# Pairing the jobs on both sides of a change of token halves, asking for sums a step ahead, and landing the first gated sums in a freed quarter

## The chip, the cores and the metric

The kernel runs on one core of a Trainium2 chip. The metric is the device time of one execution in microseconds (us), as the median of several executions. Before the change it is 2456.3 us, median of 3 (2455.7 to 2457.65).

## What is computed

One decoder block on x of shape (2048, 1024), everything in float32. A normalized and modulated h goes through one projection `z = h @ w_in`, whose columns are split into two branches. Branch A takes two column blocks a and b, forms `u = a * sigmoid(b)`, runs a causal depthwise convolution of 31 taps over the tokens, a layer norm and a SiLU, and multiplies by a gate. Branch B is windowed attention with three dilations, whose outputs are merged by weights, multiplied by a gate `silu(g_attn)` and projected by `w_attn_out`. Both branches are projected to 1024 channels, merged by sigmoid gates from further columns of z, projected by `w_out`, and added to x.

```python
z = h @ w_in
a, b, g_conv, q, k, v, g_attn, m_conv, m_attn = split(z)
u = silu(layer_norm(depthwise_causal_conv(a * sigmoid(b)))) * silu(g_conv)
o = merge(dilated_window_attention(q, k, v)) * silu(g_attn)
y = sigmoid(m_conv) * (u @ w_conv_out) + sigmoid(m_attn) * (o @ w_attn_out)
x = x + gate * (y @ w_out)
```

## The kernel before, in words

Every float32 product is made of three matmuls: each operand is split into a high part (`nc.scalar.activation(h, raw, AF.Copy)` on ACT, rounded) and a low part (raw minus high, on DVE or POOL), and high*high, high*low and low*high are added in PSUM. h itself is kept as 16 quarter tiles, a high and a low part of 4 blocks of 128 channels by 512 tokens each, named by channel half kh and token quarter t (`quarter_tile`, L224). They lie in two pools: t = 0 in a pool that lives to the end, t > 0 in one that is closed after the quads.

Four stages follow one another. The order of PE's instructions is written out by hand. The other engines' instructions are ordered by a scheduler that follows the program order as a priority but runs an instruction earlier where its inputs and its buffer are there; at run time each engine and each DMA queue works strictly in the order that came out. All DMAs concerned here are issued by SP.

1. Attention units (`project_step`, up to 1093 us).
2. Merge steps (the loop `for step, (half, j) in enumerate(order)`, L842, up to about 1211 us): 32 steps of 24 matmuls into `pzg` (L367), with the gate on ACT and DVE (`sg`, L510, L511), weights and sums of the attention outputs (`om`, L505, L507), a product on POOL (`sg`, L512), and a transpose on PE one or two steps later (`pta`, L517). In the last twelve steps, 32 pieces of 256 tokens of precomputed sums (S2, S3, S4, S1, from `s_d`) are also loaded into `raw`, a tag with three buffers, and split into the quarters of h that are no longer needed (`quarter_place`: load L830, high part on ACT L836, low part on DVE or POOL L837).
3. Quads (`quad`, `ab_quad`, `gate_quad`, about 1211 to 1987 us): a Strassen-like scheme, seven products in place of eight. There are 20 jobs for each half of the tokens; each has 7 products of 12 matmuls of 512 columns (L958), each from its own quarter (A11, A12, S2, S1, S3, S4, A22, in this order). PSUM sums go out through `kept` (ACT, L964, into one of eight scratch buffers), additions on DVE (L971, L985) and POOL (L982), and a sink: a gate job applies its function on ACT and writes to DRAM (L1081, L1082); its last result goes through a tile `gt` of which there are three. An ab job writes `ut`, from which the convolution is computed by DVE in 49 parts (`conv_parts`), taken from the list `conv_todo` by `run_conv`. The weights of the next job (`column_steps`: four loads `wB`, differences on POOL L922, high parts L927, low parts L928) are made one step per product, seven products ahead. In the last job of the first half the seven quarters are reloaded one by one: after product n, quarter n of the second half is asked for in four pieces of 512 tokens (`landing`: three pieces in the `gt` buffers and one in `ld`, or, for every other quarter, four in scratch), and split one product later. `load_wa` loads and splits the attention output weights in the last job, through `fraw`, two buffers.
4. The attention output projection `ya` (32 blocks of 12 matmuls, L1185), then the convolution branch `yc` and the output. The first block needs the four gated sums of the first 512 tokens (`ai_0`, `load_ai(0, k)`, L1261); before, they are loaded after the quads' pools are closed, through raw buffers that lie where the convolution's tiles were, and through one `gt` buffer.

Of the kernel before, what the change touches and what calls it, by code (L numbers as in the profile page):

```python
# [10 lines left out]
F32 = mybir.dt.float32  # L11
F32R = mybir.dt.float32r
# [42 lines left out]
def tile_hybrid_block(  # L55
# [168 lines left out]
    def quarter_tile(kh, t, hl, name, dtype=F32R):  # L224

        return hpools[t > 0].tile([P, 4, 512], dtype, tag=f"h{hl}{kh}{t}", name=name)

# [610 lines left out]

    def quarter_place(*args):
        quarter_load(*args[:5])  # L840
        quarter_split(*args)

    placing = [(n, k, c) for n in ("S2", "S3", "S4", "S1") for k in range(4) for c in (0, 256)]
    wts = [cur, None]
# [30 lines left out]
    ws = wpool_c.__enter__()  # L875
    wraw_c = tc.tile_pool(name="wr", bufs=7, side="right", reuse_waits="tile")
    wr = wraw_c.__enter__()
# [14 lines left out]

    def scratch(n=None):

        i = turn_of[0] % 8 if n is None else (turn_of[0] - 1) // 4 * 4 % 8 ^ 4 | n
        if n is None:
            turn_of[0] += 1
        return spares[i // 4][:, i % 4]

    def landing(i):  # L900

        if i % 8 >= 4:
            return scratch(i % 4)
        own, tag = (gp, "gt") if i % 8 < 3 else (cv, "ld")
        return own.tile([P, 512], F32, tag=tag, name=f"landing{i}", bufs=3 if tag == "gt" else 1)

# [40 lines left out]

    def quad(name, got, sink, after):

# [18 lines left out]
        s1 = kept(pa)  # L968
        after(0)
        product(1, pb)  # L970
        nc.vector.tensor_tensor(s1, s1, pb, op=ALU.add)  # L971
        sink(0, 0, s1)
        after(1)
        product(2, pa, True)
        s2 = kept(pa)
        after(2)
        product(3, pc, True)
        s5 = kept(pc)
        after(3)
# [3 lines left out]
        after(4)  # L983
# [4 lines left out]
        after(5)  # L988
        product(6, pa)
        sink(1, 0, pa)  # L990
        after(6)

    def conv_parts(half, cb, ut):

        e, o, both = ut[:, 0], ut[:, 1], cv.tile([P, 528], F32, tag="us", name=f"us{half}_{cb}")
        box = {}
# [26 lines left out]
        def join():  # L1023
            y = box["y"] = cv.tile([P, 512, 2], F32, tag="ca", name=f"ca{half}_{cb}")
            nc.vector.tensor_add(y[:, 1:, 0], box["e"][:, 1:], box["o"][:, :511])
# [7 lines left out]
        def mixed(j):  # L1033
            def f():
                dst = box["y"][:, :, 1] if j == HT else box["e"]
                stt(dst, both[:, 1 + j : 513 + j], pair_taps[:, cb, j : j + 1], box["e"], op0=ALU.mult,  # L1036
                    op1=ALU.subtract if j == 0 else ALU.add)
            return f
# [9 lines left out]

        nc.gpsimd.tensor_add(both[:, 1:], e[:, 1:], o[:, 1:])
        if half == 0:  # L1050
            nc.gpsimd.tensor_copy(tail[:, cb], ut[:, :, 513:528])
        return [*[even(j) for j in range(HT + 1)], *[odd(j) for j in range(HT)], join,
                *[mixed(j) for j in range(HT + 1)], done]

    def ab_quad(half, cb, got, after):
        ut = cv.tile([P, 2, 528], F32, tag="ut", name=f"ut{half}_{cb}")
# [16 lines left out]

        quad(f"ab{half}_{cb}", got, sink, after)

    def gate_quad(half, dst, func, cb, got, after):
        def sink(t, col, z):
# [5 lines left out]

        quad(f"g{half}_{dst.name}_{cb}", got, sink, after)

# [36 lines left out]

    got, steps = job_columns(0)
    for f in steps:
        f()
    held = []
    for i, (kind, half, g, cb) in enumerate(jobs):
        last_of_half = i + 1 < len(jobs) and jobs[i + 1][1] > half
        nxt, steps = job_columns(i + 1) if i + 1 < len(jobs) else ([], [])
        if i + 1 == len(jobs):  # L1130
            run_conv(len(conv_todo))

        def after(n):
            if steps:
                steps[n]()
            for f in held:
                f()
            held.clear()
            if last_of_half:
                name = PRODUCTS[n][0]  # L1140
                for k in range(4):
                    args = 1, name, k, slice(0, 512), landing(4 * n + k)
                    quarter_load(*args)
                    held.append(lambda args=args, k=k: quarter_split(*args, nc.gpsimd if k == 3 else nc.vector))
            else:
                run_conv(3 if n < 5 else 4)
            if i + 1 == len(jobs) and 0 < n <= NH:
                load_wa(n - 1)

        if kind is ab_quad:  # L1150
            ab_quad(half, cb, got, after)
        else:
            gate_quad(half, g[1], g[2], cb, got, after)
        got = nxt
    cv_c.__exit__(None, None, None)
# [104 lines left out]

    ais = {}  # L1261

    def load_ai(t, k):
        ais[t, k] = parts(t // 2, f"ai{t}_{k}")
        raw = gp.tile([P, 512], F32, tag="gt", name="airaw") if t == 0 and k == 3 else None
        split_big(*ais[t, k], ai_d[k, :, 512 * t : 512 * t + 512], raw=raw)

# [6 lines left out]
    def load_wc0(k):  # L1274
        load_wc(0, k, *(wcp.tile([P, 512], F32R, name=f"wc0{hl}{k}") for hl in "hl"))

    for k in range(NH):
        load_ai(0, k)
# [126 lines left out]
```

## Time and profile before

| | us |
|---|---|
| median of 3 executions | 2456.3 |
| the profiled execution: device time | 2458.03 |
| its span, first to last instruction | 2455.9 |
| PE busy | 2401.1 (98%) |
| DVE busy | 1702.4 (69%) |
| ACT busy | 970.0 (39%) |
| POOL busy | 833.3 (34%) |
| merge steps 20 to 31 with their tail, about | 1161 to 1211 |
| quads | 1211 to 1987 |

PE is the engine that is busy nearly all the time, so the time is the sum of its work and its idle pieces; a matmul of 512 columns is issued every 0.23 us at the full clock. The granted clock of PE is a share of 2.4 GHz; 0.5 is the lower of its two levels.

### The profile page before, as it was taken

How to read it: one execution, taken by the hardware profiler on the slowest of the kernel's cores; microseconds unless marked ns; L12 is line 12 of the kernel's file. 1: busy time of each engine (PE TensorE's matmuls, PEld its weight loads, DVE VectorE, ACT ScalarE, POOL GpSimd, SP SyncE). 2: the span in 40 equal slices, each digit the busy share in tenths (PEclk: the TensorE clock that was granted, in tenths of full speed). 3: DMA queues.
4: the chain of work that ended last, by engine and by line, in shares of the span. 5: the costliest groups of instructions: out<-in, count | busy, mean ns of one | idle time of the engine just before them, and what ended most of it. 6: DMA issues, size and time to landing. Idle time of an engine off the chain costs nothing.

```text
span 2455.9 us, 39171 instructions
## 1 busy us (share of the span) xinstructions
PE 2401.1 (98%) x12881; PEld 2140.9 (87%) x12881; DVE 1702.4 (69%) x3916; ACT 970.0 (39%) x2738; POOL 833.3 (34%) x954
## 2 busy tenths in 40 slices
PE   6999999999999999999899999999999999999999
PEld 2989999999999999999788888778888878888887
DVE  5855655555556555557599999999999967874333
ACT  4733433343344344335444444544444434431000
POOL 4421111111111111112486777787777710000000
PEclk8999999999999999999999999999999999999999
DMA  7633543454452221126623332542333279866343
GB/s 255 216 110 109 164 122 100 148 147 144 144 148 81 69 80 49 31 59 190 186 90 99 95 103 90 169 145 86 108 95 96 98 278 315 269 198 221 121 147 101
DMA packets 329737, 336.26 MB, mean 137 GB/s; under 512 B 27512, under 2 KB 251032, under 8 KB 329534
## 3 DMA queue, kind: packets, MB, share of 16 engines
q1 hardware_dynamic: 327758, 331.07, 42.9%
q10 hardware_dynamic: 1776, 2.69, 0.3%
q8 instruction: 103, 1.69, 0.3%
q14 instruction: 100, 0.82, 0.1%
HBM read 216.01 MB, written 117.64 MB: 136 GB/s over the span
## 4 chain that ended last, share of the span: by engine, by line
PE 89%; DMA 3%; ACT 2%; DVE 1%; POOL 1%; issue 1%; SPq 0%; DVEq 0%; POOLq 0%; ACTq 0%
PE pz L367 30%; PE yc L1185 7%; PE out L1185 7%; PE paab L958 7%; PE ya L1185 4%; PE pcab L958 4%; PE pag_mc_d L958 4%; PE pag_g_d L958 4%; PE pag_ma_d L958 3%; PE ps L439 3%; PE po L458 3%; PE pcg_g_d L958 2%; PE pcg_mc_d L958 2%; PE ptq L429 2%; PE pzg L367 2%; PE pbab L958 2%
## 5 line engine op out<-in xcount | busy, mean ns | idle before, releaser
L367 PE MATMUL pz<-wh_u,hT_lo 128*128 128x384 f32 x1536 | 538.5, 351 | 4.9 <-DVE hT_lo L286 2.7
L367 PE MATMUL pz<-wh_u,hT_hi 128*128 128x384 f32 x1536 | 519.6, 338 | 6.3 <-ACT wh_u L343 3.3
L367 PE MATMUL pz<-wl_u,hT_hi 128*128 128x384 f32 x1536 | 520.4, 339 | 0.5 <-DVE wl_u L346 0.4
L395 DVE SCALAR_TENSOR_TENSOR qk<-pz,st,wqk 128x128 f32<-128x128 f32 x384 | 117.0, 346 | 319.9 <-POOL st L111 319.7
L110 POOL TENSOR_SCALAR st<-st 128x2 f32<-128x2 f32 x192 | 48.1, 251 | 815.5 <-ACT sq L384 815.5
L367 PEld LDWEIGHTS pz<-wh_u,hT_hi 128*128 128x128 f32 x1536 | 291.7, 190 | 9.0 <-ACT wh_u L343 4.0
L367 PEld LDWEIGHTS pz<-wh_u,hT_lo 128*128 128x128 f32 x1536 | 290.1, 189 | 8.0 <-DVE hT_lo L286 3.5
L367 PEld LDWEIGHTS pz<-wl_u,hT_hi 128*128 128x128 f32 x1536 | 290.6, 189 | 2.1 <-DVE wl_u L346 1.6
L431 ACT ACTIVATE qkT<-ptq 128x256 f32<-128x256 f32 x192 | 73.6, 383 | 420.6 <-PE ptq L429 420.0
L928 POOL TENSOR_TENSOR slT<-wB,shT 128x512 fp32r<-128x512 f32 x120 | 163.1, 1367 | 55.8 <-ACT shT L927 55.8
L1036 DVE SCALAR_TENSOR_TENSOR ce<-us,pair_taps,ce 128x512 f32<-128x512 f32 x240 | 179.6, 749 | 1.5
L1007 DVE SCALAR_TENSOR_TENSOR ce<-ut,chan,ce 128x512 f32<-128x512 f32 x240 | 179.3, 747 | 0.0
L1020 DVE SCALAR_TENSOR_TENSOR cq<-ut,chan,cq 128x512 f32<-128x512 f32 x208 | 156.3, 752 | 3.8
L384 ACT ACTIVATE sq<-pz 128x128 bf16<-128x128 f32 x384 | 106.0, 276 | 100.8 <-PE pz L367 93.9
L111 POOL TENSOR_TENSOR st<-st,mhalf 128x2 f32<-128x2 f32 x192 | 136.5, 711 | 16.0
L927 ACT ACTIVATE shB<-wB 128x512 fp32r<-128x512 f32 x120 | 75.6, 631 | 155.6 <-issue 111.7
L922 POOL TENSOR_TENSOR wB<-wB,wB 128x512 f32<-128x512 f32 x80 | 105.0, 1313 | 45.3 <-DVE slB L928 40.4
L444 ACT ACTIVATE sm<-sm,osb 128x128 f32<-128x128 f32 (+1 forms) x192 | 88.7, 462 | 62.4 <-DVE osb L442 59.6
L927 ACT ACTIVATE shT<-wB 128x512 fp32r<-128x512 f32 x120 | 75.1, 626 | 87.5 <-PE pcab L958 24.4
L1368 DVE TENSOR_TENSOR ot<-out,gate_row 128x512 f32<-128x512 f32 x32 | 22.1, 692 | 116.2 <-PE out L1185 116.2
L458 PE MATMUL po<-lv,pT 128*128 128x128 f32 x600 | 97.3, 274 | 0.0
L458 PEld LDWEIGHTS po<-lv,pT 128*128 128x128 f32 x600 | 93.1, 189 | 0.5 <-issue 0.5
(610 smaller groups left out, 6336.6 us busy)
## 6 DMA issues: line engine op xcount, KB each, us to landing
wB<-in_w_in_dram SPq DMA_DIRECT2D x160, 256.0 KB, 3.4
qkv_d<-qkv SPq DMA_DIRECT2D x128, 192.0 KB, 2.3
raw_u<-in_w_in_dram SPq DMA_DIRECT2D x93, 192.0 KB, 2.8
lqk<-qkv_d SPq DMA_DIRECT2D x128, 128.0 KB, 2.3
acc_d<-osb SPq DMA_DIRECT2D x192, 65.0 KB, 1.7
at<-acc_d SPq DMA_DIRECT2D x64, 195.0 KB, 3.9
wada<-in_w_ada_dram SPq DMA_DIRECT2D x16, 512.0 KB, 8.4
lv<-qkv_d SPq DMA_DIRECT2D x128, 64.0 KB, 1.9
```

The lines of the kernel that those rows point to most:

```text
L111: nc.gpsimd.tensor_tensor(dst, scratch[:, :n], mhalf[:, :n], op=ALU.pow)
L367: nc.tensor.matmul(pz[:, :width], part(a, k, P * j, P), w[:, :width], start=(m == 0), stop=(m == 23))
L384: nc.scalar.activation(sq, pz[:, P * i : P * i + P], AF.Square, scale=1.0 / math.sqrt(P), accum_out=st[:, i : i + 1])
L395: nc.vector.scalar_tensor_tensor(qk[:, 2 * i : 2 * i + 2].rearrange("p a b -> p (a b)"), pz[:, P * i : P * i + P], st[:, 2 + i : 3 + i], w ...
L458: nc.tensor.matmul(po[:, :P], box["pT"][:, P * i : P * i + P], vt, start=(i == 0), stop=(i == nk - 1))
L927: nc.scalar.activation(h, q[name], AF.Copy)
L928: eng.tensor_tensor(l, q[name], h.bitcast(F32), op=ALU.subtract)
L958: nc.tensor.matmul(ps, w, x, start=(m == 0 and ps.name not in first), stop=(m == 11 and not more), skip_group_check=True)
L1007: stt(box["e"], e[:, 1 + j : 513 + j], chan[:, cb, 2 * j : 2 * j + 1], box["e"], op0=ALU.mult, op1=ALU.add)
L1020: stt(box["o"], o[:, 2 + j : 514 + j], w, psum_o, op0=ALU.mult, op1=ALU.add)
L1036: stt(dst, both[:, 1 + j : 513 + j], pair_taps[:, cb, j : j + 1], box["e"], op0=ALU.mult, op1=ALU.subtract if j == 0 else ALU.add)
L1185: nc.tensor.matmul(pz, w, xx, start=(m == 0), stop=(m == len(terms) - 1))
```

## The change

- `quarter_tile` puts the quarter (kh, t) = (0, 2) into the pool that lives to the end.
- Merge steps: `quarter_place` is taken apart. Each of the steps 19 to 30 only loads its pieces, into `raw` (three buffers, odd steps) or into a new tag `sl` (three buffers, even steps); the split comes in the following step, after that step's `merge_step`.
- Quads: jobs 18 and 19 (the last two of the first half) and jobs 20 and 21 (the first two of the second) run in pairs, product by product: product 0 of both, product 1 of both, and so on. `quad` becomes a generator, `prepare` makes weight steps seven slots ahead in the new order, raw weight buffers go from 7 to 10. In job 19 the quarters are loaded after each of its products, all through the three `gt` buffers and `ld`, and split two slots later. The other jobs stay single. `run_conv` takes 2 parts per slot in the first pair, elsewhere 3 or 4. `us` and `ca` of the convolution have one buffer in place of two, and the sum for `us` becomes a part of its own.
- The first gated sums `ai0` are loaded in the last job, after products 3 to 6, through `fraw`, into the quarter of S2; `wc0` k = 4 to 7 later uses the same quarter, in place of own tiles.

```diff
-        if step >= 20:
-            for i, (n, k, c0) in enumerate([placing.pop(0) for _ in range(3 if step < 28 else 2)]):
-                raw = wp.tile([P, 384], F32, tag="raw", name=f"raw{n}_{k}_{c0}", bufs=3)[:, :256]
-                quarter_place(0, n, k, slice(c0, c0 + 256), raw, nc.vector if i < 2 else nc.gpsimd)
+        landed, landing = landing, []
+        if 19 <= step < 31:
+            for i, (n, k, c0) in enumerate([placing.pop(0) for _ in range(3 if step < 27 else 2)]):
+                if step % 2:
+                    raw = wp.tile([P, 384], F32, tag="raw", name=f"raw{n}_{k}_{c0}", bufs=3)[:, :256]
+                else:
+                    raw = wk.tile([P, 256], F32, tag="sl", name=f"sl{n}_{k}_{c0}", bufs=3)
+                landing.append((0, n, k, slice(c0, c0 + 256), raw))
+                quarter_load(*landing[-1])
...
         turns += merge_step(half, j, pz, state)
+        for i, args in enumerate(landed):
+            quarter_split(*args, nc.vector if i < 2 else nc.gpsimd)
...
+    def load_ai0(k):
+
+        if k == 0:
+            big["ai0"] = [quarter_tile(0, 2, hl, f"ai0{hl}") for hl in ("hi", "lo")]
+        ais[0, k] = [x[:, k] for x in big["ai0"]]
+        split_big(*ais[0, k], ai_d[k, :, :512])
...
+    for group in [*[[i] for i in range(half_jobs - 2)], [half_jobs - 2, half_jobs - 1], [half_jobs, half_jobs + 1],
+                  *[[i] for i in range(half_jobs + 2, len(jobs))]]:
+        slots += [(i, n) for n in range(7) for i in group]
...
+    for at, (i, n) in enumerate(slots):
+        if n == 0:
+            kind, *job = jobs[i]
+            running[i] = kind(*job, columns[i][0])
+        next(running[i], None)
+        prepare(at + 7)
+        while held and held[0][0] <= at:
+            held.pop(0)[1]()
+        if i == half_jobs - 1:
+            for k in range(4):
+                own, tag = (gp, "gt") if k < 3 else (cv, "ld")
+                raw = own.tile([P, 512], F32, tag=tag, name=f"landing{n}_{k}", bufs=3 if k < 3 else 1)
+                args = 1, PRODUCTS[n][0], k, slice(0, 512), raw
+                quarter_load(*args)
+                held.append((at + 2, lambda args=args, k=k: quarter_split(*args, nc.gpsimd if k == 3 else nc.vector)))
+        run_conv(2 if half_jobs - 2 <= i < half_jobs else 3 if n < 5 else 4)
         if i + 1 == len(jobs):
-            run_conv(len(conv_todo))
...
+            if 0 < n <= NH:
                 load_wa(n - 1)
+            if n > 2:
+                load_ai0(n - 3)
```

## Rows read from the trace of the kernel before

**Rows 1.** Waits of PE, whole run: line, releaser, us in total, times, longest

```profile
PE pta L517 <- POOL sg L512: 11.2, 8, 2.5
PE paab L958 <- ACT spare_hi L964: 3.4, 1, 3.4
PE pag_ma_d L958 <- ACT spare_lo L964: 2.8, 1, 2.8
```

**Rows 2.** Windows: stretch, length, busy us (instructions) by engine, clock, DMA share, GB/s

```profile
1161.00:1211.00 50.00, 40.62 (x331) 39.10 (x329) 35.77 (x123) 26.48 (x86) 15.72 (x20) 1.00 0.57 178
1576.00:1625.00 49.00, 42.83 (x169) 34.38 (x169) 45.08 (x46) 30.45 (x56) 41.00 (x28) 0.90 0.73 227
1625.00:1968.00 343.00, 343.00 (x1515) 284.17 (x1515) 329.70 (x483) 145.12 (x257) 249.73 (x195) 1.00 0.30 96
```

**Rows 3.** Waits of ACT, 1146 to 1209 us

```profile
ACT S_hi L836 <- DMA rawS<-s_d: 12.6, 12, 2.1
```

**Rows 4.** DMA issues, 1146 to 1209 us: count, size, median us to landing

```profile
rawS<-s_d SPq DMA_DIRECT2D x29, 128.0 KB, 4.1
```

**Rows 5.** Timeline in the merge steps: start, us, instruction [idle before, releaser]

```profile
1130.17 0.32 SPq L830 DMA_DIRECT2D rawS<-s_d  x1
...
1156.29 1.11 ACT L836 ACTIVATE S_hi<-rawS 128x256 fp32r<-128x256 f32 x3 [1.97 <-DMA rawS<-s_d]
...
1210.51 0.44 PE L517 MATMUL pta<-ident,sg 128*128 128x128 f32 x2 [1.57 <-POOL sg L512]
```

**Rows 6.** Chain of waits, 1573 to 1612 us and the whole run: start, us, what

```profile
1590.31 4.61 PE pag_ma_d L958 x12
1594.91 2.73 PE pcg_ma_d L958 x12
...
1609.20 5.49 PE paab L958 x12
```

**Rows 7.** Timeline of the change of halves, ACT, SP and DVE

```profile
1577.05 0.58 ACT L1081 ACTIVATE gt<-pag_ma_d 128x512 f32<-128x512 f32 x1
...
1581.95 1.68 ACT L836 ACTIVATE A_hi<-landing 128x512 fp32r<-128x512 f32 x3 [1.60 <-DMA landing<-h_d]
...
1584.02 2.81 SPq L830 DMA_DIRECT2D landing<-s_d  x3
...
1586.62 5.14 DVE L837 TENSOR_TENSOR A_lo<-spare_hi,A_hi 128x512 fp32r<-128x512 f32 x3
...
1590.16 1.66 ACT L836 ACTIVATE S_hi<-landing 128x512 fp32r<-128x512 f32 x3
...
1604.79 0.60 ACT L1081 ACTIVATE gt<-pag_ma_d 128x512 f32<-128x512 f32 x1
...
1605.28 0.68 DVE L837 TENSOR_TENSOR S_lo<-landing,S_hi 128x512 fp32r<-128x512 f32 x1
```

**Rows 8.** DMA issues, 1576 to 1625 us

```profile
landing<-s_d SPq DMA_DIRECT2D x8, 256.0 KB, 3.9
```

**Rows 9.** Timeline: `fraw` early, then the last job and the start of ya

```profile
1214.42 0.85 SPq L1105 DMA_DIRECT2D fraw<-in_w_attn_out_dram  x2
...
1971.63 1.15 ACT L1106 ACTIVATE wah<-fraw 128x512 fp32r<-128x512 f32 x2
...
1982.11 1.23 DVE L1047 TENSOR_TENSOR usum<-usum,ca 128x1024 f32<-128x1024 f32 x1
...
1984.74 0.63 ACT L1106 ACTIVATE wah<-fraw 128x512 fp32r<-128x512 f32 x1 [1.54 <-DMA fraw<-in_w_attn_out_dram]
1984.90 0.42 SPq L1105 DMA_DIRECT2D fraw<-ai_d  x1
...
1987.59 0.63 ACT L1106 ACTIVATE wah<-fraw 128x512 fp32r<-128x512 f32 x1 [1.19 <-DMA fraw<-in_w_attn_out_dram]
...
1989.80 0.55 PE L1185 MATMUL ya<-ai_0h,wah 128*128 128x512 f32 x1 [2.38 <-ACT ai_0h L1106]
...
1999.17 0.40 PE L1185 MATMUL ya<-ai_0h,wah 128*128 128x512 f32 x1
```

More of the change, by code (lines that the diff above doesn't have):

```diff
@@ L891, in tile_hybrid_block, with scratch @@
     spares = [quarter_tile(1, 3, hl, f"spare_{hl}", F32) for hl in ("hi", "lo")]
[L893 to L897, printed above, removed]
+    def scratch():
+        i = turn_of[0] % 8
+        turn_of[0] += 1
         return spares[i // 4][:, i % 4]
[L900 to L905, printed above, removed]
     def run_conv(count):
@@ L946, in column_steps, with quad @@
         return got, [lambda n=n: step(n) for n in range(7)]
-    def quad(name, got, sink, after):
+    def quad(name, got, sink):
         pa, pb, pc = bank("z", f"pa{name}"), bank("s", f"pb{name}"), bank("o", f"pc{name}")
@@ L968, in quad @@
         s1 = kept(pa)
-        after(0)
+        yield
         product(1, pb)
@@ L982, in quad @@
         nc.gpsimd.tensor_tensor(s3, s3, s5, op=ALU.add)
-        after(4)
+        yield
         product(5, pc)
@@ L987, in quad @@
         sink(1, 1, s3)
-        after(5)
+        yield
         product(6, pa)
         sink(1, 0, pa)
-        after(6)
+        yield
     def conv_parts(half, cb, ut):
-        e, o, both = ut[:, 0], ut[:, 1], cv.tile([P, 528], F32, tag="us", name=f"us{half}_{cb}")
+        e, o = ut[:, 0], ut[:, 1]
         box = {}
@@ L1023, in join @@
         def join():
-            y = box["y"] = cv.tile([P, 512, 2], F32, tag="ca", name=f"ca{half}_{cb}")
+            y = box["y"] = cv.tile([P, 512, 2], F32, tag="ca", name=f"ca{half}_{cb}", bufs=1)
             nc.vector.tensor_add(y[:, 1:, 0], box["e"][:, 1:], box["o"][:, :511])
@@ L1047, in done, with add, ab_quad @@
                 nc.vector.tensor_add(usum[:, tsl], usum[:, tsl], y)
-        nc.gpsimd.tensor_add(both[:, 1:], e[:, 1:], o[:, 1:])
+        def add():
+            both = box["both"] = cv.tile([P, 528], F32, tag="us", name=f"us{half}_{cb}", bufs=1)
+            nc.gpsimd.tensor_add(both[:, 1:], e[:, 1:], o[:, 1:])
         if half == 0:
             nc.gpsimd.tensor_copy(tail[:, cb], ut[:, :, 513:528])
-        return [*[even(j) for j in range(HT + 1)], *[odd(j) for j in range(HT)], join,
+        return [*[even(j) for j in range(HT + 1)], add, *[odd(j) for j in range(HT)], join,
                 *[mixed(j) for j in range(HT + 1)], done]
-    def ab_quad(half, cb, got, after):
+    def ab_quad(half, _, cb, got):
         ut = cv.tile([P, 2, 528], F32, tag="ut", name=f"ut{half}_{cb}")
@@ L1072, in sink, with gate_quad @@
                 conv_todo.extend(conv_parts(half, cb, ut))
-        quad(f"ab{half}_{cb}", got, sink, after)
-    def gate_quad(half, dst, func, cb, got, after):
+        return quad(f"ab{half}_{cb}", got, sink)
+    def gate_quad(half, g, cb, got):
+        _, dst, func = g
         def sink(t, col, z):
@@ L1082, in sink @@
             nc.sync.dma_start(dst[cb + col, :, 1024 * half + 512 * t : 1024 * half + 512 * t + 512], th)
-        quad(f"g{half}_{dst.name}_{cb}", got, sink, after)
+        return quad(f"g{half}_{dst.name}_{cb}", got, sink)
     jobs = []
@@ L1121, in load_wa @@
             split_big(wh[k][:, sl], wl[k][:, sl], w_attn_out[P * k : P * k + P, sl], nc.gpsimd if c0 else nc.vector)
[L1123 to L1129, printed above, removed]
-        if i + 1 == len(jobs):
-            run_conv(len(conv_todo))
[L1133 to L1147, printed above, removed]
-                load_wa(n - 1)
[L1150 to L1154, printed above, removed]
@@ new lines, in tile_hybrid_block @@
+    ais = {}
+    def load_ai0(k):
[3 more added lines that the diff above has]
+        split_big(*ais[0, k], ai_d[k, :, :512])
+    half_jobs = len(jobs) // 2
+    slots = []
+    for group in [*[[i] for i in range(half_jobs - 2)], [half_jobs - 2, half_jobs - 1], [half_jobs, half_jobs + 1],
+                  *[[i] for i in range(half_jobs + 2, len(jobs))]]:
+        slots += [(i, n) for n in range(7) for i in group]
@@ new lines, in tile_hybrid_block, with prepare @@
+    columns, running, held = {}, {}, []
+    def prepare(at):
+        for i, n in slots[at : at + 1]:
+            if n == 0:
+                columns[i] = job_columns(i)
+            columns[i][1][n]()
+    for at in range(7):
+        prepare(at)
+    for at, (i, n) in enumerate(slots):
+        if n == 0:
+            kind, *job = jobs[i]
[12 more added lines that the diff above has]
+        run_conv(2 if half_jobs - 2 <= i < half_jobs else 3 if n < 5 else 4)
+        if i + 1 == len(jobs):
+            if 0 < n <= NH:
+                load_wa(n - 1)
+            if n > 2:
+                load_ai0(n - 3)
@@ L1155, in tile_hybrid_block @@
+    assert not conv_todo
     cv_c.__exit__(None, None, None)
@@ L1259, in plan_norm @@
             at_block(at, m, f)
-    ais = {}
     def load_ai(t, k):
         ais[t, k] = parts(t // 2, f"ai{t}_{k}")
-        raw = gp.tile([P, 512], F32, tag="gt", name="airaw") if t == 0 and k == 3 else None
-        split_big(*ais[t, k], ai_d[k, :, 512 * t : 512 * t + 512], raw=raw)
+        split_big(*ais[t, k], ai_d[k, :, 512 * t : 512 * t + 512])
     wc = [[None] * KC, [None] * KC]
```

24 lines of the change are left out of this document (12 added, 12 removed).

## The prediction

> **What bounds the kernel now.** I read the waits of PE first, because PE is busy 98% of the span: what PE waits for is nearly all that can be won. Three stretches carry what this change touches. In the merge steps PE waits 11.2 us in 8 places for POOL's `sg` before a transpose; around the change of halves it waits 2.8 and 3.4 us for ACT's `kept` [rows 1]; at the first block of ya 2.4 us for `ai_0` [rows 9]. Then the windows give each stretch its whole loss. From 1161 to 1211, 50.0 less 40.62 busy: 9.4 us idle. From 1576 to 1625, 6.2 us idle at a mean granted clock of 0.90, while 1625 to 1968 shows 343.00 busy of 343 [rows 2]. So single jobs away from these places lose nothing.
>
> After each of the two idle pieces of the change of halves the clock falls for a while to its lower level: a product of 12 matmuls takes 4.61 and 5.49 in place of 2.73 [rows 6], 4.6 us more. The change of halves thus costs 6.2 + 4.6 = 10.8 us. At the start of ya, PE is free at 1989.80 - 2.38 = 1987.4; two blocks of 12 matmuls, 2.73 each [rows 6], would be done at 1992.9, and the third block starts at 1999.17 [rows 9]: 6.3 us lost. All three together, 26.5 us, are the most that the change can give.
>
> One more engine has to be watched: from 1625 to 1968 DVE is busy 329.70 of 343 [rows 2], 96%, so it is nearly a second bound.
>
> **Part 1, sums a step ahead.** What delays `sg`: ACT stands in its queue before `S_hi`, waiting for the piece from DRAM, 12 times and 12.6 us [rows 3], for instance 1.97 us at 1156.29 [rows 5]; the gate and `om` behind it come late, then DVE and POOL, then PE (up to 2.5 at once [rows 1]). That the load stands a step earlier in the program does little by itself: the first `rawS` load is issued at 1130 [rows 5], ten steps before its place in the program, as soon as a `raw` buffer is free. What helps is six buffers for three. A piece takes 4.1 us to land [rows 4], and the waits come once for each refill of the buffers. S2 and S3, S4, and S1 each wait for a quarter of h to come free; with six buffers the first six of each of these three groups have landed by then, 18 of 32 pieces, and the other 14 come in 2 + 1 + 1 = 4 refills where 12 waits are seen. The last idle piece, 1.57 at 1210.51 [rows 5], belongs to the last step's own chain and stays. (9.4 - 1.6) x 4/12 + 1.6 = 4.2 remain: **5.2 us gained**. Bounds: 0, if ACT meets each piece as early as now; 7.8, if only the tail stays. The loads themselves are as many as now and cost SP the same.
>
> **Part 2, pairs.** PE's instructions are the same. Quarter n is now given free after both jobs' product n and wanted 14 slots later in place of 7 products less one, 35 us in place of 16. An eviction (`kept`) has three slots of 2.72 (2.73 [rows 6] but for the rounding) before PE wants its bank again, in place of one; so late ACT work inside the pairs is hidden by 8 us. What is late next is the border between the pairs. Job 18's last result goes through a `gt` buffer, and only then is its PSUM bank free, which job 20 needs one slot later (two banks of this tag, both in use in a pair). The `gt` buffers now also carry three of the four pieces of every quarter. They seem to be handed out in program order: the first landing into `gt` comes right behind job 18's `gt` [rows 7], while `fraw`, with no such rival, is filled at 1214, 750 us ahead of its use [rows 9]. Then job 18's result must wait until the first piece of quarter 5 has been split.
>
> The turn of one landing buffer: 3.9 us to land [rows 8], 0.4 for the issue, 0.6 for ACT (1.68 for three), and for DVE 0.68 alone or 5.14/3 = 1.7 beside POOL [rows 7]: 5.6 to 6.6, and I take 6.5, since POOL is nearly always busy here (41.00 of 49 [rows 2]). The first split comes 5.5 us after the pair's start (two slots), the sixth 5 x 6.5 later, its end 2.0 later, job 18's sink 0.6 later: 40.6. The bank is wanted at 14 x 2.72 = 38.1. So PE stops for 2.5 us; the idle piece of 2.5 in the merge steps [rows 1] passed at a granted clock of 1.00 [rows 2], so I add none. **10.8 - 2.5 = 8.3 us gained**. Bounds: 10.8 gained with a turn of 5.6; with the longest turn that the trace shows, 1581.95 to 1590.16 = 8.2 us [rows 7], 5.5 + 41 + 2.6 - 38.1 = 11.0 of idle time and 1.9 of lower clock, 2.1 lost.
>
> The weights of a pair need 28 POOL instructions with the quarter pieces, as the window 1576 to 1625 has them: 41.00 us [rows 2] for 38.1. POOL falls some 3 us behind; weights are made seven slots, 19 us, ahead, which hides it; uncovered it would be a stop of 3. More `wr` buffers and the single `us` and `ca` I cost at nothing: 16 and more parts of the convolution lie between two uses of `us` or `ca` and cover them; without that cover DVE would stop for one instruction, some 0.7 (329.70/483 [rows 2]).
>
> The Trainium skill, on "SBUF — State Buffer" (section "Who interferes with whom"), has a rule that speaks against this part: a DVE instruction with two SBUF inputs and a POOL instruction that reads SBUF hold a shared port pair exclusively, for their whole length. The trace nearly agrees: DVE's low part is 0.68 alone and 1.7 in the crowd [rows 7], and 1.28 of POOL (249.73/195 [rows 2]) with 0.68 would make 1.96 in line. By that rule the pair's 28 POOL and some 25 such DVE instructions would stand in one line; the time that gives is the third rival's.
>
> **Part 3, `ai0` through `fraw`.** Before, these loads begin at 1984.90, once the convolution's memory is free, into four buffers [rows 9]. Now they stand among the eight pieces of the attention weights, twelve through two buffers. The first splits come at 1971.63 (two, at 0.5 distance), the fourth of each buffer at 1984.74 and 1987.59 [rows 9]: turns of 4.4 (low part on DVE) and 5.1 (on POOL). In the new order the third and fourth `ai0` pieces are the sixth of each buffer: 1984.74 + 4.4 + 5.1 = 1994.2, and 1987.59 + 4.4 + 4.4 = 1996.4, plus 1.3 for the two parts: 1997.7. PE can begin the first block at once, then stops until the second piece at about 1992, runs at the lower clock, ends the block at about 1998.5 and the second, partly at the lower clock, 3.4 later (between 2.73 and 5.49 [rows 6]), at 2001.9, where 1999.17 was before: **2.7 us lost**. Bounds: 6.3 gained if the pieces come in time; 6 lost if each of the six turns is half a microsecond longer.
>
> **Part 4, DVE at the end.** The last convolution ends at 1982.11 + 1.23 = 1983.3 [rows 9], 4.1 before the quads end. DVE's work does not shrink, the quads do by 8.3; the convolution then ends some 4 us after the quads, and the low parts for ya share DVE with it: **1.0 us lost** (bounds 0 and 4). The evictions of ya have six banks, 6 x 2.73 = 16 us, as cover; beyond it PE would wait for each further microsecond.
>
> The sum: -5.2 - 8.3 + 2.7 + 1.0 = -9.8. The profiled execution took 2458.0 (span 2455.9 and 2.1 around it) and would be 2448.2; it lies 1.7 above the median of 2456.3, so the median goes to **2446.5**.
>
> **Rivals.**
> (a) All three stretches close: turns of 5.6, `ai0` in half the time: -7.8 - 10.8 - 3 = -21.6, 2435. For it: single jobs run without a gap. Against: DVE at 96% [rows 2].
> (b) The merge steps don't change, because loads and splits were already run ahead of the program: -4.6, 2452. For it: the issue at 1130 [rows 5]. Against: three more buffers.
> (c) The landing turn is 7.6 to 8: 28 POOL instructions of 1.28 and 25 of DVE of 0.68, one after the other, are 53 us for seven quarters, 7.6 each. The stop at the border is 5.5 + 38 + 2.6 - 38.1 = 8 us and 1.9 of clock: part 2 gives 0.9, the sum is -2.4, 2454. For it: the 1.7 [rows 7]. Against: most DVE and POOL instructions of the pair are not at work at the same time.
> (d) Slower: the same place with a turn over 9. At 8.2, seen above, the sum is +0.6; it decides from there. At 9.2 the stop is 16 us and 1.9 of clock, part 2 loses 7.1, the sum is +5.6, 2462. For it: DVE and POOL both full, and one set of four buffers where two sets were. Against: in the seen turn of 8.2, convolution parts and two sets shared DVE and DMA; eight parts of it are left here.
>
> **How the numbers follow.** Forecast 0.42 (its own range 2440 to 2452), (a) 0.12, (b) 0.15, (c) 0.19, (d) 0.12. A measurement of this kernel can tell 0.2%, 4.9 us, from no change. Faster by more: 0.40 of the forecast's 0.42, all of (a), half of (b), 0.02 of (c): 0.62. Within: the rest of these, 0.02 + 0.07 + 0.15 = 0.24. Slower: 0.02 of (c), (d): 0.14. The range 2434 to 2459 leaves out the ends of (a) and (d).
>
> **What would show it.** Part 1: ACT's waits for the sums' pieces fall from 12.6 to about 4, PE's for `sg` from 11.2 to about 5. Part 2: no PE wait for `kept` at the change of halves; one wait of 2 to 3 us at the first product of job 20, and job 18's `gt` activation right behind a split of S4. Part 3: the third block of ya starts 14 to 15 us after the quads end (11.8 before), with waits for `ai0` behind the first. Wrong would be: PE waits in the pairs for weights or `kept`, a stop at the border over 5 us, or merge steps with as much idle time as now.

## The result, and the profile after

The kernel after takes 2463.66 us (median of 9; 2460.95 to 2465.9), the kernel before 2456.91 beside it (median of 9): ratio 1.0027, 95% interval [1.0017, 1.0037], so 6.75 us slower where 9.8 less had been forecast. The profiled executions, 2461.91 (span 2460.1) against 2458.03 (2455.9), show 4.2 us of it in the span. The difference sits in four stretches, two better and two worse. First the windows of the kernel before, then of the kernel after: the merge steps from the sixteenth on with the first quad's start; jobs 18 to 21; from the last job's start to the third ya block; ya blocks 8 to 15. Columns are length, busy us (instructions) of PE, PE's weight loads, DVE, ACT and POOL, clock, DMA share, GB/s.

```profile
1146.06:1211.52 65.46, 54.73 (x448) 53.01 (x447) 47.95 (x163) 35.31 (x113) 20.63 (x26) 1.00 0.58 180
1557.45:1644.54 87.09, 80.92 (x338) 65.94 (x336) 80.07 (x98) 47.62 (x86) 69.17 (x49) 0.94 0.57 177
1968.22:1999.17 30.95, 28.34 (x109) 21.86 (x108) 18.06 (x25) 12.16 (x21) 6.80 (x5) 0.89 0.64 216
2016.89:2042.00 25.11, 25.11 (x116) 20.27 (x115) 17.39 (x29) 9.68 (x17) 1.65 (x2) 1.00 0.93 314
```

```profile
1144.02:1206.86 62.84, 56.29 (x449) 54.52 (x447) 48.99 (x163) 36.09 (x113) 20.95 (x26) 0.96 0.58 180
1553.01:1637.52 84.51, 78.32 (x337) 64.34 (x336) 62.57 (x79) 48.59 (x87) 66.33 (x47) 0.96 0.61 185
1961.20:1999.51 38.31, 28.84 (x110) 21.52 (x108) 31.11 (x44) 12.44 (x22) 7.09 (x6) 0.82 0.69 223
2016.74:2046.21 29.47, 27.19 (x115) 21.11 (x114) 21.20 (x35) 11.08 (x19) 1.28 (x2) 0.94 0.94 319
```

By length: -2.6, -2.6, +7.4, +4.4, together +6.5. The first 1146 us came out 2.0 shorter, though the change touches nothing there, and the remaining pieces (ya blocks 2 to 7 -0.5, the first quads +0.2) make up the rest to +4.2. Read the DVE column (the third busy figure) downwards: 80.07 became 62.57 in jobs 18 to 21, 18.06 became 31.11 in the last job and the first ya blocks, 17.39 became 21.20 in ya. The counts say it more plainly: 98 DVE instructions became 79 in jobs 18 to 21, and 25 became 44 in the last job and the first ya blocks. Some 19 DVE instructions, 17.5 us of its busy time, are missing at the change of halves and come at the end, some 400 us later.

PE's waits, whole run, beside [rows 1]:

```profile
PE ya L1200 <- ACT ai0hi L1106: 9.4, 2, 5.0
...
PE paab L953 <- ACT gt L1081: 6.2, 1, 6.2
PE pta L517 <- POOL sg L512: 6.0, 6, 2.2
...
PE paab L953 <- ACT shB L922: 1.6, 1, 1.6
PE ya L1200 <- ACT ai_2h L1106: 1.5, 1, 1.5
...
PE ya L1200 <- DVE ai_2l L1107: 0.8, 1, 0.8
```

In the merge steps ACT's wait for the sums' pieces fell from 12.6 us in twelve [rows 3] to 2.6 in eight in the same stretch (1144 to 1207 here; 2.1 for `raw`, 0.5 for `sl`). One more wait of 1.8, before `om`, is put down to a piece too; with it, it is about the 4 that was forecast. PE's own wait for `sg` fell only to 6.0.

At the change of halves the two waits for `kept` are gone and one stop stands at the first product of job 20. All engines, in order of time, lines left out at the dots (compare [rows 7]):

```profile
1591.19 1.71 POOL L977 TENSOR_TENSOR spare_lo<-spare_lo 128x512 f32<-128x512 f32 x1
...
1595.24 0.63 ACT L836 ACTIVATE S_hi<-landing 128x512 fp32r<-128x512 f32 x1 [0.64 <-DMA landing<-s_d]
1595.26 1.09 DVE L837 TENSOR_TENSOR S_lo<-landing,S_hi 128x512 fp32r<-128x512 f32 x1
...
1596.82 0.57 ACT L1081 ACTIVATE gt<-pag_ma_d 128x512 f32<-128x512 f32 x1
...
1597.44 0.79 PE L953 MATMUL paab<-A_hi,shB 128*128 128x512 f32 x1 [6.19 <-ACT gt L1081]
```

The `gt` activation follows a split of S4, as forecast (between the two ACT makes two high parts of weights, until 1596.9); PE waits 6.19 us. The first row is POOL's `s3 += s5` of job 19, whose operand ACT had copied out at 1583.71: POOL is some 7 us behind as well. In this stop the granted clock falls to its lower level, from 1594.59 for 6.83 us.

At the end (ACT, SP's queue and DVE, beside [rows 9]):

```profile
1983.90 0.47 SPq L1216 DMA_DIRECT2D d<-u_d  x1
1985.14 0.32 SPq L1105 DMA_DIRECT2D fraw<-ai_d  x1
1985.43 0.63 ACT L1106 ACTIVATE ai0hi<-fraw 128x512 fp32r<-128x512 f32 x1 [1.66 <-DMA fraw<-ai_d]
...
1991.73 0.63 ACT L1106 ACTIVATE ai0hi<-fraw 128x512 fp32r<-128x512 f32 x1 [5.67 <-DMA fraw<-ai_d]
...
1993.77 0.63 ACT L1106 ACTIVATE ai0hi<-fraw 128x512 fp32r<-128x512 f32 x1 [1.41 <-DMA fraw<-ai_d]
...
1997.41 1.23 DVE L1042 TENSOR_TENSOR usum<-usum,ca 128x1024 f32<-128x1024 f32 x1
```

The quads end at 1980.24. Three of the four `ai0` pieces come after it, and the third block starts at 1999.51, 19.3 later (11.9 before). The last part of the convolution ends at 1998.64, 18.4 after the quads; before it ended 4 us ahead of their end [rows 9]. The piece asked for at 1985.14 takes 6.6 us to land beside the 512 KB loads of `d`.

### The profile page after: what moved, and what is told of

Its sections match the earlier page's. It is cut to its first block, busy times and chain, and to the rows that moved or that the text cites. A ratio compares the mean times of both kernels' runs of the same rounds, so it can differ in the third digit from the quotient of the medians.

```text
span 2460.1 us, 39180 instructions
## 1 busy us (share of the span) xinstructions
PE 2402.9 (98%) x12881; PEld 2141.1 (87%) x12881; DVE 1696.2 (69%) x3916; ACT 973.1 (40%) x2738; POOL 839.6 (34%) x954
## 4 chain that ended last, share of the span: by engine, by line
PE 88%; DMA 4%; DVE 2%; ACT 1%; POOL 1%; issue 1%; SPq 0%; DVEq 0%; POOLq 0%; ACTq 0%
PE pz L367 30%; PE yc L1200 7%; PE out L1200 7%; PE paab L953 7%; PE pag_g_d L953 4%; PE pcab L953 4%; PE pag_mc_d L953 4%; PE ya L1200 3%; PE ps L439 3%; PE po L458 3%; PE pag_ma_d L953 2%; PE pzg L367 2%; PE pcg_mc_d L953 2%; PE pcg_g_d L953 2%; PE ptq L429 2%; PE pbab L953 2%
```

## The experiments

Two theories after the result. **P**: three places, each by itself, as the prediction had them (a stop at the border, two raw buffers for `ai0`, a slightly later convolution). **D**: the pairs starve DVE at the change of halves; the late convolution then delays all at the end.

### Parts alone

The kernel before with the sums' pieces a step ahead (`quarter_load` one step before `quarter_split`, six raw buffers); with the pairs only; with `ai0` through `fraw` only.

> The kernel before with the first part alone: sums' pieces asked for a step ahead, six raw buffers for three. Theory P (three separate places): the merge steps from step 15 to the last matmul shrink by 3 to 4 us as in the changed kernel (62.4 to 58.8), some 1 us is given back at the lower clock of the first quad, the rest is as before: -2 to -4 us, about 2453.5. Rival D (DVE, below) says the same here. A third possibility, that the later splits delay the first quads' S quarters, would show as PE waits for S_lo or S_hi in the first job and 0 or a loss.

2456.64, ratio 0.9996 [0.9987, 1.0005]. The steps from 15 to the last matmul took 59.2 us in place of 62.4: 3.2 us, not to be told in the median. The largest of PE's waits in this stretch, and ACT's for the pieces:

```profile
PE pta L517 <- POOL sg L512: 6.8, 7, 1.8
```

```profile
ACT S_hi L836 <- DMA rawS<-s_d: 2.9, 6, 1.2
...
ACT S_hi L836 <- DMA slS<-s_d: 1.6, 3, 0.7
```

> The changed kernel without its first and third part: pairs alone (with ten raw weight buffers and single us and ca). Theory P: quads 2 to 3 us shorter than before, a stop of about 6 us at job 20 behind job 18's gt tile, ya begins as before: -2 to -3 us, 2454. Rival D (in the second pair the ab job hands over its ut only at slot 13, DVE runs dry for some 19 us and ends the convolution some 18 us after the quads, in place of 4 us before their end): since ai_0 here waits for the convolution's memory, ya begins 15 to 20 us later than before, against quads 2.6 shorter: +12 to +18 us, about 2470.

2474.78, ratio 1.007 [1.0053, 1.0087]: the pairs alone lose 17 us.

```profile
PE ya L1193 <- ACT ai_0h L1101: 23.1, 1, 23.1
PE paab L948 <- ACT gt L1076: 5.8, 1, 5.8
```

The convolution ends 11.8 us after the quads. Here `ai_0` lands where its tiles were, so PE waits 23.1 us for it. D's sign and size hold for the pairs by themselves (17 us lost, 12 to 18 expected), though the convolution is less late than the 18 us that D gave; the stop at the border is there too.

> The kernel before with the third part alone: ai_0 through the two fraw buffers among the attention output weights' pieces, into the quarter of S2. Theory P (two buffers for twelve pieces): the third block of ya starts 15 to 19 us after the quads' end in place of 11.9, +3 to +7 us, about 2461. Rival D (the late convolution is what delays ya, and the buffers are harmless): the convolution ends 4 us before the quads here, so ya's third block comes as before or up to 3 us earlier: 2453 to 2457.

2466.61, ratio 1.0034 [1.0021, 1.0047], with a convolution that ends 4 us ahead of the quads' end: the third block starts 23.4 us after that end.

```profile
PE ya L1196 <- ACT ai0hi L1106: 12.7, 3, 7.7
```

So part 3 alone costs some 11.5 us of the path, and DVE can't be the reason. Both theories hold, at one place each.

### The end: convolution and raw buffers

```diff
-[half_jobs - 2, half_jobs - 1], [half_jobs, half_jobs + 1], *[[i] for i in range(half_jobs + 2, len(jobs))]
+[half_jobs - 2, half_jobs - 1], *[[i] for i in range(half_jobs, len(jobs))]
```

> The kernel after, with the second pair taken apart: jobs 18 and 19 stay a pair, 20 and 21 run one after the other. Theory D (VectorE runs dry after the change of halves because two jobs in a pair hand their first convolution over only after 13 products; it idles 19.6 us of 1591 to 1637.5 in the kernel after and 3.0 in the kernel before): the convolution's last part starts at most 6 us after the last matmul of the quads in place of 18.4, the waits of ya's eighth block for ai_2 (2.3 us) go, and the 29.5 us from ya's block 8 to block 16 are 25 to 26; 3 to 5 us faster than the kernel after from this alone. Theory P (each place by itself, the late end of the convolution has another cause): that stretch stays above 28. Both: the one stop at the change of halves stays, 5 to 7 us, and the gap ahead of ya's third block shrinks by no more than 3 us.

2462.92, ratio 1.003 [1.0018, 1.0042]: no gain over the kernel after. Windows of jobs 18 to 21, of the last job to the third block, of ya blocks 8 to 15:

```profile
1553.13:1638.63 85.50, 78.26 (x337) 63.82 (x336) 78.19 (x98) 48.46 (x87) 67.16 (x47) 0.96 0.58 180
1962.32:2004.38 42.06, 29.67 (x109) 22.13 (x108) 21.84 (x31) 15.73 (x27) 7.20 (x6) 0.80 0.73 249
2021.62:2046.73 25.11, 25.11 (x116) 20.25 (x114) 17.84 (x30) 9.62 (x17) 1.27 (x2) 1.00 0.95 319
```

D is confirmed in what it says of DVE: it is busy 78.19 us again, the convolution ends 3.9 us ahead of the quads' end, and blocks 8 to 15 take 25.11. But the stretch before it grew from 38.31 to 42.06, which neither theory had. SP's queue and ACT show why:

```profile
1981.33 0.94 SPq L1105 DMA_DIRECT2D fraw<-ai_d  x2
1982.31 0.49 SPq L1105 DMA_DIRECT2D fraw<-in_w_conv_out_dram  x1
1982.90 0.39 SPq L1105 DMA_DIRECT2D fraw<-ai_d  x1
...
1986.07 0.32 SPq L1105 DMA_DIRECT2D fraw<-ai_d  x1
...
1991.35 0.33 SPq L1105 DMA_DIRECT2D fraw<-ai_d  x1
```

```profile
1989.97 0.63 ACT L1106 ACTIVATE ai0hi<-fraw 128x512 fp32r<-128x512 f32 x1 [4.78 <-DMA fraw<-ai_d]
...
1992.96 0.63 ACT L1106 ACTIVATE ai0hi<-fraw 128x512 fp32r<-128x512 f32 x1 [0.80 <-DMA fraw<-ai_d]
1997.81 0.63 ACT L1106 ACTIVATE ai0hi<-fraw 128x512 fp32r<-128x512 f32 x1 [4.21 <-DMA fraw<-ai_d]
```

The early end of the convolution frees memory, and loads for the second 512 tokens (`ai_0h`, `ai_1h`) and for `wc0` are issued at 1981 to 1982, ahead of the last three pieces of the first 512, which still wait for their two buffers. These are issued at 1982.90, 1986.07 and 1991.35 and take 6.5 to 7.1 us each.

```diff
-        split_big(*ais[0, k], ai_d[k, :, :512])
+        own, tag = (gp, "gt") if k < 3 else (cv, "ld")
+        raw = own.tile([P, 512], F32, tag=tag, name=f"airaw{k}", bufs=3 if k < 3 else 1)
+        split_big(*ais[0, k], ai_d[k, :, :512], raw=raw)
```

> The kernel after, with the four gated sums ai0 landing in the three gt buffers and ld (all idle by then) in place of the two fraw buffers that the attention output weights use. Theory P (the third ya block is late because the four pieces queue for two buffers): the third block starts 8 to 13 us after the quads' last matmul in place of 19.3, the waits for ai0 (9.4 us in two) are below 3 us, and the time is 5 to 9 us below the kernel after. Theory D (it is late because VectorE still has the convolution): pieces are there early on ScalarE but the low parts are not, the third block still starts 17 us or more after the quads' end.

2455.93, ratio 0.9994 [0.9985, 1.0004]: 7.7 us below the kernel after, P's range. From the last job's start to the third block 26.4 us in place of 38.3 (24.5 are 108 matmuls at the full clock). But then:

```profile
PE ya L1202 <- DVE yt L1316: 6.5, 1, 6.5
```

The convolution still ends 19 us after the quads, and PE now stops for evictions of ya that DVE makes behind it. Each cause hides behind the other; so both were taken away at once:

> The kernel after, with jobs 20 and 21 one after the other, and ai0 landing in gt and ld. Theory DP (the late convolution and the two fraw buffers are two causes of one late stretch, so that either alone brings nothing or half): third ya block 3 to 7 us after the quads' last matmul (19.3 in the kernel after, 3.6 with ai0 in gt alone), the wait of 6.5 us for yt goes, 17 to 18 us from ya's block 2 to block 8 and 25 to 26 from 8 to 16: 14 to 18 us below the kernel after, 2445 to 2449. Rival: the earlier end of the convolution lets the next loads start earlier and these delay ai0 in gt as well (as they did fraw with one pair): third block 12 us or more after the quads' end, 2453 or more.

**2448.26, ratio 0.9963 [0.9951, 0.9975]**: 15.4 us below the kernel after and 8.4 below the kernel before.

```profile
1553.61:1640.94 87.33, 78.81 (x338) 64.42 (x336) 77.66 (x100) 48.48 (x87) 66.14 (x47) 0.94 0.58 179
1964.62:1990.95 26.33, 24.81 (x110) 20.19 (x108) 17.62 (x25) 12.51 (x22) 6.50 (x6) 1.00 0.60 181
```

The third block comes 26.33 us after the last job's start, the clock stays at its full level there, and the wait for `yt` is down to 0.8. Jobs 18 to 21 take 87.33, no less than before (87.09), and the stop at the border is still there, the longest of these kernels so far:

```profile
PE paab L953 <- ACT gt L1081: 7.9, 1, 7.9
```

The same without any pair, that is the kernel before with parts 1 and 3 alone and `ai0` in `gt` and `ld`:

> The kernel before with the sums' pieces a step ahead and ai0 landing in gt and ld in the last job; no pairs. Theory: the merge's 3.2 us and a third ya block 3 to 7 us after the quads' end in place of 11.9: 8 to 12 us below the kernel before, 2445 to 2448, so that the pairs as they stand bring 0 to 3 us. Rival: without the pairs' later loads the landing buffers and the gt results of the last jobs collide with ai0, third block at 10 us or more, 2452 or more.

2450.46, ratio 0.9974 [0.9963, 0.9986].

```profile
1551.69:1637.79 86.10, 78.39 (x338) 64.04 (x336) 79.00 (x97) 47.03 (x85) 69.28 (x49) 0.98 0.59 182
1961.47:1986.67 25.20, 24.77 (x109) 20.19 (x108) 17.38 (x24) 12.04 (x22) 6.42 (x5) 1.00 0.60 180
```

The two intervals overlap: the first pair by itself brings nothing that can be told. In these two profiles jobs 18 to 21 are 1.2 us shorter without it, but single profiles differ by more: with the first pair alone and the landing as in the kernel after these jobs take 85.5 and 87.3 us, with no pair 86.1 to 87.7 in four profiles. Only with both pairs are they clearly below, 84.3 to 84.7 in four.

### The stop at the border

Jobs 18 and 19 put their last result into one of the eight scratch buffers (`th = s5`), not into `gt`:

> The changed kernel, but a gate job's last result goes through its own scratch buffer s5, which is free by then, so that the sinks and the landing quarters share no buffers. Theory P (the stop at job 20 is the wait of job 18's sink for a gt buffer that holds a piece of quarter 5): the stop of 6.2 us and the lower clock behind it (about 2 us) go, quads about 8 us shorter than in the changed kernel. If instead DVE and POOL in each other's way cause it, whatever the buffers, a stop of 4 us or more stays. Rival D: DVE has as much work as before, so the convolution then ends some 26 us after the quads in place of 18, and a part of the 8 us is given back in ya: 2458 to 2463, against 2455.5 by theory P.

2463.04, ratio 1.0021 [1.0009, 1.0033]; the stop stays.

```profile
PE paab L953 <- ACT spare_lo L1081: 6.7, 1, 6.7
```

The order of the `gt` buffers alone does not hold it. POOL adds `s5` of job 18 at 1590.53 for 1.74 us, so its buffer is free at 1592.3; yet ACT puts out job 18's last result only at 1598.94, behind splits of landing pieces (the last at 1597.88, after 0.56 us of waiting for its piece) and sinks whose sums DVE adds late (1595.13, 0.52 us of waiting).

> The kernel after, with POOL relieved around the change of halves: the low parts of the weights of jobs 18 and 19, the addition s3 += s5 of these two jobs and the fourth pieces of the landing go to VectorE. Theory E (POOL has more work there than time, some 29 instructions of 1.3 to 1.7 us in 38 us, and runs 10 us late; ScalarE waits behind it): the stop of 6.2 us at the first product of job 20 falls below 2 us, 4 to 7 us faster than the kernel after. Theory L (the landing's turn sets it: a load, a split and the next load in the same four buffers take 7.1 us for a quarter where two products take 5.5): the stop stays at 5 us or more.

2467.47, ratio 1.005 [1.0035, 1.0065].

```profile
PE paab L953 <- ACT gt L1082: 11.1, 1, 11.1
```

Worse by 4 to 5 us. The edit missed the two additions (it asked for the two jobs by a name that they don't have); they still ran on POOL, at 1585.83 and 1592.17, so it tests only the splits: with the landing's fourth pieces and the low parts on DVE, the stop grows.

> The kernel after, where only pieces 0 and 1 of each quarter of the second half are loaded, and pieces 2 and 3 are split from the same two buffers (their own data are left out; every split is there). Theory L (the landing's turn): 14 loads in place of 28 through buffers that are handed over half as often, the stop at the first product of job 20 falls below 2 us. Theory E (POOL is late): the stop stays at 5 us or more, as POOL has every instruction that it had.

2462.57, ratio 1.0025 [1.0014, 1.0037]; the stop is 5.2 us. Half the loads take one microsecond off, little against the spread of the stop (5.7 to 7.9 us in five profiles that leave the first pair and its landing as in the kernel after). So the number of loads is not what holds it. The landing's buffers are not excluded by this run: each is now held for two splits, `gt` still takes 14 pieces in place of 21, and ACT still waits 3.7 us at once for a piece (1586.23).

Another candidate is order: ACT and DVE, each in its own order, stand at landing splits that nobody wants before slot 22.

```diff
+    LAND_AT = (1, 3, 5, 7, 13, 15, 17)
-        if i == half_jobs - 1:
+        past = at - slots.index((half_jobs - 2, 0))
+        if past in LAND_AT:
+            q = LAND_AT.index(past)
```

> The kernel after, with the landing of quarters 4 to 6 (S3, S4, A22) asked for at slots 13, 15 and 17 in place of 9, 11 and 13, so behind the last results of jobs 18 and 19 in program order; they are wanted at slots 22, 24 and 26. Theory O (order: on ScalarE and VectorE, which work in order, splits that are wanted some 25 us later stand in front of the additions and of the gt result that free the bank for job 20): the stop of 6.2 us at job 20's first product falls below 1.5 us, its lower clock (6.8 us at half speed) goes too, the 84.5 us from job 18 to job 22 become 75 to 78, and the time is 6 to 9 us below the kernel after. Theory W (work: VectorE and POOL have more to do in this stretch than time): the stop only moves, and stops of 5 us or more in sum come at later products of jobs 20 and 21.

```profile
PE paab L953 <- ACT gt L1081: 3.4, 1, 3.4
```

The stop falls by 2.8 us, jobs 18 to 21 from 84.5 to 81.9: about half of what O gave the stop and a third of what it gave the stretch. The time, 2463.41 (1.003 [1.0016, 1.0043]), shows none of it: it is within what the runs scatter (2457.15 to 2469.44), and the late end stays. Two more tries at the other 3.4 us: `s3 += s5` on DVE on top (`own = nc.vector if name[:7] == "g0_ma_d" and name[-2:] in ("_4", "_6") else nc.gpsimd`), and convolution parts put off (`run_conv(2 if n < 3 else 0)` in the first pair).

> The kernel after with the landing of quarters 4 to 6 later (slots 13, 15, 17) and the addition s3 += s5 of jobs 18 and 19 on VectorE in place of POOL; nothing else moves. Theory O2 (what is left of the stop, 3.4 us, is POOL in order: the two additions run some 6 us after their operands behind copies and weight differences, and ScalarE, in order, waits 1.8 us for them ahead of gt): the stop falls below 1.5 us and job 18 to job 22 takes 77 to 79 us in place of 81.9. Theory W (VectorE is as late as POOL there): stop 3 us or more, 81 us or more.

> The kernel after with the landing of quarters 4 to 6 later (slots 13, 15, 17) and, in the first pair, two convolution parts a slot only up to product 2 and none from product 3 on (they run later, in the stretch where VectorE idles 19.6 us). Theory W (VectorE is behind: the additions s2 += pcg wait in order behind convolution parts, and ScalarE's gt result waits in order behind the sinks of these sums): the stop of 3.4 us falls below 1.5, job 18 to job 22 takes 77 to 79.5 us in place of 81.9. Theory O3 (order on ScalarE and the landing loads alone): the stop stays at 3 us or more.

2464.66 (1.0035 [1.0022, 1.0047]) and 2464.03 (1.0035 [1.0021, 1.0049]), jobs 18 to 21 in 85.0 and 82.6 us, stops of

```profile
PE paab L953 <- ACT gt L1082: 4.2, 1, 4.2
```

```profile
PE paab L953 <- ACT gt L1081: 4.3, 1, 4.3
```

With the additions on DVE, ACT waits 4.3 us for them there in place of 1.8 for POOL: DVE is at least as late, as W said. The second try did not do what it should: DVE's order in its trace still has convolution parts in front of the additions,

```profile
1589.88 3.12 DVE L1031 SCALAR_TENSOR_TENSOR ce<-us,pair_taps,ce 128x512 f32<-128x512 f32 x4
1592.90 0.68 DVE L980 TENSOR_TENSOR spare_hi<-spare_hi,pcg_ma_d 128x512 f32<-128x512 f32 x1
```

probably because the scheduler runs them ahead of their place in the program. It is inconclusive. So about half of the stop goes with the place of the landing: the six profiles with the later landing, here and below, have stops of 2.5 to 4.3 us, those of the kernel after and its variants without it 5.2 to 11.1. The edit moves the loads, their buffers' turns and the splits at once; with `gt` left out of the sink the stop stayed, which speaks for the splits' order on ACT and DVE. What holds the other half, work on DVE or order on ACT, stays open.

The later landing, and the two further edits, in the version that beats both kernels:

> The same as the one before with the landing of quarters 4 to 6 later as well (slots 13, 15, 17). Theory O: 5 to 9 us below the kernel with one pair and ai0 in gt. Theory W, or the single job 20 that wants quarters 4 to 6 at slots 18 to 20 where they land at about 16 to 21: the stop comes back as waits of 3 to 6 us at the last products of job 20, and the time stays within 3 us of that kernel.

> The same two edits on the kernel with one pair and ai0 in gt and ld. Theory O2: the stop of 2.45 us goes, the waits at the last products of job 20 (3.5 us in five) stay; 2 to 4 us below the version without the edit, some 2446 to 2448. Theory W: within 1.5 us of that version.

> The same edit in the version with one pair, ai0 in gt and ld and the landing later (2449.9 measured, stop 2.45 us and 3.5 us of waits in job 20). Theory W: stop below 1 us, 2446 to 2448.5. Rival: the convolution parts put off collide with the single job 20, whose splits VectorE must make: waits in job 20 grow to 5 us or more, and the time stays at 2449 or more.

2449.91 (0.9974 [0.9965, 0.9983]), 2448.28 (0.9963 [0.995, 0.9976]) and 2451.46 (0.9983 [0.9973, 0.9992]). The first two can't be told from the version without them (2448.26, 0.9963 [0.9951, 0.9975]); the third is probably slower than it, by 3 to 5 us, as its rival said (2449 or more). In the first the stop is 2.5, and PE then waits 3.5 us more in five places of the single job 20, 2.1 for quarters that now land too late and 1.4 for `kept`; jobs 18 to 21 take 89.1 us there, no less than 87.33, so W's rival for that version holds. The best that was run is one pair with `ai0` in `gt` and `ld`.

## Why the prediction was wrong

**Part 1** (-5.2): the mechanism was right, and ACT's wait for the pieces fell to about the forecast 4 (4.5 with part 1 alone, 2.6 in the kernel after). The step that failed is the size: the 9.4 idle microseconds, less the tail, were put down to these waits in proportion, but 3.2 to 3.6 was all that went with them. PE still waits 6.0 us for `sg`. Of the 3.6, 1.0 was lost again ahead of the first quad: there PE stops for 1.57 us for the high part of its weights (`shB`), and from 1205.5, within this stop, the granted clock is at its lower level for 6.8 us.

**Part 2** (-8.3): the stop came at the named place and behind the named instruction. It was 6.2 and not 2.5, with 6.8 us at the lower clock, and the stretch gained 2.6. The term that was mis-sized is the turn of a landing buffer, 6.5: the first splits of the first and the sixth quarter lie at 1559.50 and 1595.24, five turns of 7.1. Put into the forecast's own sum, 5.5 + 5 x 7.1 + 2.6 - 38.1 gives 5.5 us of stop. But that agreement doesn't prove the mechanism: without `gt` in the sink the stop stayed at 6.7, with half the loads at 5.2, and only a later place of the landing shortened it, to 3.4. Late splits, late additions and the order on ACT stand in one chain; with one of them taken away the next one still holds PE. POOL's lag, which the forecast put at some 3 us and hid, was 7 at the last addition. DVE's low part took 0.68 to 1.78 us (median 1.12) in this stretch:

```profile
L837 DVE TENSOR_TENSOR S_lo<-landing,S_hi x12: 678/1117/1780, 1574.9 to 1596.9; 128x512 fp32r<-128x512 f32 x12
```

The Trainium skill's rule of a port pair that one of the two engines holds for a whole instruction ("SBUF — State Buffer", section "Who interferes with whom") agrees with that spread. Rival (c), with a turn of 7.6 to 8 and a stop of 8 us, came nearer than the forecast.

**Part 4** (+1.0) is the step that failed in kind. It let the convolution end some 4 us after the quads, because "DVE's work does not shrink, the quads do". That takes DVE as always fed. Job 20, the ab job of the second pair, hands its convolution over only at the 13th slot in place of the 7th, and the list runs empty. DVE's largest waits in jobs 20 and 21, first in the kernel after (1591 to 1637.5), then before (1595.5 to 1644.5):

```profile
DVE spare_hi L980 <- PE pcab L953: 9.7, 1, 9.7
DVE slB L923 <- ACT shB L922: 5.2, 1, 5.2
```

```profile
DVE ut L1069 <- ACT spare_hi L1065: 2.5, 1, 2.5
```

Most of the idle time of an engine that is 96% busy for the next 343 us [rows 2] comes back at the end. From the start of job 18 to the end of the convolution it is 425.9 us before and 439.1 with the pairs alone: 13.2 more for the 17.0 us that DVE was less busy in jobs 18 to 21 (63.09 for 80.07). In the kernel after it is 445.6, and the convolution ended 18.4 us after the quads. Most of the further 6.6 belongs to part 3: DVE, in its own order, stands 3.3 us before late `ai0` pieces and splits them between the convolution's parts. From block 8 on ya waited for `ai_2` (1.5 and 0.8 us, with the lower clock), since these pieces land where the convolution's tiles were: +4.4. With jobs 20 and 21 single this went to nothing (25.11 again, in the kernel whose convolution ends 3.9 us before the quads), and with `ai0` in buffers of its own it was worth 7.7 us of the time (2455.93 to 2448.26). The prediction had the 96% in hand and asked only whether DVE's work grows, not whether the new order keeps it supplied.

**Part 3** (+2.7, bounds to 6 lost): the two buffers were the cause, as forecast, and the size was off: +7.4 beside the change, +11.5 alone. The turns of 4.4 and 5.1 were read from loads in a quiet stretch (median 2.7 us from issue to landing for the weights there, before and after); among the 512 KB loads of `d` the last two pieces took 6.6 and 7.0 us. Without the two buffers this place took 25.2 to 26.4 us, where 24.5 is the least.

The sum by span: -2.6 for -5.2, -2.6 for -8.3, +7.4 for +2.7, +4.4 for +1.0. Rival (d), the slower one, gave the sign and nearly the time (2462) for another reason: it put the loss at the border, where in fact 2.6 were won. That it came near is luck.

## What to carry to other kernels

When an order of work is changed to give one engine's waits more slack, ask which engine lives on the results in the old order: a second engine that is 96% busy pays back most of its idle microseconds at the end of its stretch (13.2 of 17.0 here). A late stretch can have two causes that hide each other; single experiments then look like failures (-0.7 and -7.7 us here), and only both together show what there is (-15.4). Loads that are needed first should have buffers of their own: with two shared ones, in the kernel with one pair, they were overtaken by loads that were needed some 17 us later (the time of ya's blocks 2 to 7).

## What was not expected of the hardware

A 256 KB load took 2.7 us from issue to landing (median of six loads of weights in the last job of the kernel after) and 6.6 and 7.0 us when it was issued at 1985.14 and 1986.81, beside 512 KB loads and with the DMA engines 0.96 busy (1980.24 to 1999.51). In the chain of ACT, DVE and POOL at the border one 128x512 subtraction cost DVE from 0.68 to 1.78 us and POOL from 1.29 to 2.28, while the convolution's instructions, whose running sum lies in PSUM, stayed at 0.74 to 0.78 in the same stretch. With the stop of 6.2 us PE had the lower clock for 6.8 us; with the one of 3.4 us, in the kernel that lands later, for 3.4. But the length of the stop alone does not give it: a stop of 5.2 us (half the loads) went with 3.4, one of 4.2 (additions on DVE) with 6.8, and one of 3.4, in the version with one pair, the later landing and the additions on DVE, with none.
